# Exchange of the rotary halves: four ScalarE copies out of PSUM in place of four DMAs per half tile

## Chip, cores and metric

One Trainium2 chip, one of its cores. The time is the device time of one execution in microseconds (us); a run's time is that of the slowest core, here the only one. Each engine of the core (TensorE or PE, VectorE or DVE, ScalarE or ACT, GpSimd or POOL, and SyncE or SP, which issues the DMAs) executes its own list of instructions in order; they wait for each other by semaphores.

## What is computed

One layer of a hybrid encoder on 1024 tokens of width 1024: a mixer (window attention of 8 query heads and 2 key heads of width 64, beside a gated delta rule), cross-attention into 256 memory tokens, and a SwiGLU feed-forward net, each between norms. The change touches the rotary embedding of the queries and keys of the window attention:

```python
def _rope(x, positions):
    half = x.shape[-1] // 2                      # 32
    inv_freq = ROPE_THETA ** (-jnp.arange(half, dtype=jnp.float32) / half)
    ang = positions.astype(jnp.float32)[..., None] * inv_freq
    cos = jnp.cos(ang)[:, :, None, :]
    sin = jnp.sin(ang)[:, :, None, :]
    x1, x2 = xf[..., :half], xf[..., half:]
    return jnp.concatenate([x1 * cos - x2 * sin, x2 * cos + x1 * sin], axis=-1)
...
    aq = _rope(aq.reshape(b, s, ATTN_HEADS, ATTN_HEAD_DIM), positions)
    ak = _rope(ak.reshape(b, s, ATTN_KV_HEADS, ATTN_HEAD_DIM), positions)
    attn_o = _window_attention(aq, ak, av, attn_sink[l])
```

Each head's 64 channels are two halves of 32. Every channel is multiplied by a cosine, and the channel 32 places away, times a sine with a sign, is added.

## The kernel before

The kernel keeps activations with channels on the 128 partitions and tokens along the free axis, and works on two halves of 512 tokens (`HALF`). Weights and activations are split into a rounded part and a rest (`split`, L102 and L103), and each matrix product is three matmuls. `proj` (L263) loads one block of 128 weight columns, splits it and multiplies it with both token halves; `gemm_b` (L260) issues 24 matmuls for each half into one PSUM bank of the pool `pg`, which has three.

The first part of the kernel (to about 605 us) is the mixer. `ORDER_1` names the delta rule's projections and the inverses of its chunk triangles, whose sums run on VectorE (`base_inverse`, L510 and L512). `ORDER_2` names the stage of this case: the gate projections `G`, the level merges `L` (`levels`), the value projection `V`, the attention projections `A` and the windows `W`:

```python
ORDER_2 = "G0 G1 G2 G3 L0 L1 V A4 A0 A1 W L2 L3 W W A2 A3 W".split()
```

`A4` projects the keys, `A0` to `A3` project 128 query channels (two heads) each. `attn_proj` (L701) handles one block: for each token half VectorE multiplies the bank by the sine table into `sn` (L709) and by the cosine table into `rop` (L710). Four DMAs on SP bring `sn` to `rot` with neighbouring blocks of 32 partitions swapped (L714), since VectorE and GpSimd combine only what lies on the same partition. GpSimd adds (L715) and SP stores the sum to `d_q` or `d_k` in DRAM (L716). There are five blocks of two halves, ten rounds in all. The tiles `rop`, `rot` and `rot2` have two buffers each (`trp`). The sine table is `sinT` (L392): the sine of the angle times `rope_s`, a column of +1 and -1 that the host makes (L71).

`next_windows` starts a new window of 128 queries and finishes the one before. A window (`window`) loads keys `kr` (L610), queries `qr` (L611) and values `vr` (L613) from DRAM, splits them on ACT and GpSimd (`khi` L616, `qs` L624 and L625), forms scores (L633) with their maxima on VectorE (L635), exponentials on ACT (`sc`, L642 and L650), and in its second part transposes them (L656), splits them (`ph`, `pl`) and multiplies by the values (L661). The queries of the first eight windows come from `A0` and `A1`, those of the last eight from `A2` and `A3`.

`levels` fetches blocks of the inverses (`cz`, `cw`, L530), spreads them over tiles with ACT, VectorE and GpSimd (`m` L540, `c` L541 and L543, `D` and `Z` L553), and goes through four small products on TensorE (L569, L575), each followed by a copy on ACT (`bs` L571, `z` L580, `Z` L591) or VectorE (L592). It stores to `d_pz` (L594). When all of it is done the scan of the delta rule starts (`scan`, L749, loads at L771 and L772), interleaved with more windows by `ORDER_3`. The scan's tiles take over memory that the projections and the rotary tiles had on the right side.

Within these lists a planner decides the order: the program is traced and then each engine's instructions are put into an order by the program order, the dependences and the times that a timing model expects. The order on each engine is fixed then; on the chip an instruction whose input is late holds up everything behind it on its engine.

Of the kernel before, what the change touches and what calls it, by code (L numbers as in the profile page):

```python
# [10 lines left out]
F32 = mybir.dt.float32  # L11
# [3 lines left out]
ALU = mybir.AluOpType  # L15
# [4 lines left out]
P = 128  # L20
# [4 lines left out]
HALF = 512  # L25
# [17 lines left out]
_ROPE_AT = len(_NAMES) * P  # L43
# [3 lines left out]
def host_constants():  # L47
    i = np.arange(P)
    blk = i // 32
    a, b = i[:, None], i[None, :]  # L50
    ba, bb = blk[:, None], blk[None, :]
    tri = {
        "ident": a == b,
        "mU": a < b,
        "mL": a > b,
        "mUi": a <= b,
        "mLi": a >= b,
        "m5": (ba // 2 == bb // 2) & (ba != bb),
        "m6": ba // 2 != bb // 2,
        "ones": a + b >= 0,  # L60
    }
    out = np.zeros((P, _NCONST), np.float32)
    for n, m in tri.items():
        out[:, _AT[n]:_AT[n] + P] = m

    out[:, _AT["band0"]:_AT["band0"] + P] = np.where(b >= a, 0.0, NEG)
    out[:, _AT["band2"]:_AT["band2"] + P] = np.where(b <= a, 0.0, NEG)
    half = np.arange(32, dtype=np.float32)
    inv = np.power(np.float32(10000.0), -half / np.float32(32)).astype(np.float32)
    out[:, _ROPE_AT] = inv[i % 32]  # L70
    out[:, _ROPE_AT + 1] = np.where(i % 64 < 32, 1.0, -1.0)  # L71
    return out


# [1 line left out]
def tile_hybrid_block(  # L76
# [4 lines left out]
    g_ffn_pre, w_gate_up, w_down, g_ffn_post, consts, out, dump=None, stop=None,  # L81
):
    nc = tc.nc
    x, mem, out = x[0], mem[0], out[0]
# [23 lines left out]
    def pool(name, bufs, **kw):  # L108
        return tc.tile_pool(name=name, bufs=bufs, reuse_waits="tile", **kw)
# [37 lines left out]
    trp = p1.enter_context(pool("trp", 2, side="right"))  # L147
# [62 lines left out]
    for hf in range(2):  # L210
        hi = hx.tile([P, KT, HALF], F32R, name=f"hhi{hf}")
        lo = hx.tile([P, KT, HALF], F32R, name=f"hlo{hf}")
        for j in range(4):
# [10 lines left out]
            for kq in range(2):  # L224
# [4 lines left out]
                o = slice(4 * kq, 4 * kq + 4), slice(j * P, (j + 1) * P)  # L229
# [33 lines left out]
    def proj(src_cols, eng=None):  # L263
        whi, wlo = load_w(src_cols, KT, P, eng)
        pp = [pg.tile([P, 512], F32, tag="pg", name="pg") for _ in range(2)]
        gemm_b(whi, wlo, hT, pp)
        return pp
# [42 lines left out]
    for hf in range(2):  # L310
        pp = pg.tile([P, 512], F32, tag="pg", name="pg")
# [65 lines left out]
    sinT = rt.tile([P, S], F32, name="sinT")  # L377
    cosT = rt.tile([P, S], F32, name="cosT")
    for hf in range(2):
        sl = slice(hf * HALF, (hf + 1) * HALF)  # L380
# [320 lines left out]
    def attn_proj(ct):  # L701
        pp = proj(w_in[:, ct * P:(ct + 1) * P])
        dst = d_q[ct * P:(ct + 1) * P, :] if ct < 4 else d_k
        for hf in range(2):
            sl = slice(hf * HALF, (hf + 1) * HALF)
            rop = trp.tile([P, HALF], F32, tag="rop", name="rop")
            sn = trp.tile([P, HALF], F32, tag="rot", name="sn")
            rot = trp.tile([P, HALF], F32, tag="rot2", name="rot2")
            nc.vector.tensor_tensor(sn, pp[hf], sinT[:, sl], ALU.mult)  # L709
            nc.vector.tensor_tensor(rop, pp[hf], cosT[:, sl], ALU.mult)  # L710

            for q in range(4):
                o = 32 * (q ^ 1)
                nc.sync.dma_start(rot[32 * q:32 * q + 32], sn[o:o + 32])  # L714
            nc.gpsimd.tensor_tensor(rop, rop, rot, ALU.add)  # L715
            nc.sync.dma_start(dst[:, sl], rop)  # L716

# [13 lines left out]
    def gate_proj(h):  # L731

        pp = proj(w_in[:, 2304 + h * P:2304 + (h + 1) * P])
        for hf in range(2):
            gt = trp.tile([P, HALF], F32, tag="rop", name="gt")
            nc.scalar.activation(gt, pp[hf], AF.Silu)
            nc.sync.dma_start(d_gate[h * P:(h + 1) * P, hf * HALF:(hf + 1) * HALF], gt)

    issue(ORDER_2, {"A": attn_proj, "V": value_proj, "G": gate_proj, "L": levels, "W": next_windows})
    dump("d_q", d_q); dump("d_k", d_k); dump("d_gate", d_gate); dump("d_v", d_v)  # L740
    p1.close()
# [453 lines left out]
    def bank(name):  # L1195
        return pg.tile([P, 512], F32, tag="pg", name=name)
# [123 lines left out]
    for t in range(NT):  # L1320
        tok = slice(t * P, (t + 1) * P)
        pp = bank("pd2")
# [57 lines left out]
```

## Time and profile before

| | |
|---|---|
| median of 3 runs | 1625.35 us (1624.68 to 1629.03) |
| profiled execution, its own time | 1627.8 us |
| its span, first to last instruction | 1626.1 us |
| mean granted TensorE clock | 0.984 |
| PE busy | 1554.1 us (96%) |
| DVE busy | 940.8 us (58%) |
| ACT busy | 747.7 us (46%) |
| POOL busy | 543.8 us (33%) |

The profile is of one execution. A row of the timeline reads: start, duration, engine, line, operation, output <- input, form, count, and in brackets the idle time of the engine before it with what released it. "PEq", "SPq" and the like are the sequencers. Rows of groups give minimum, median and maximum in ns, or the busy time with the mean. PEclk is the share of full speed that TensorE's clock was granted. A busy TensorE is not one at its peak.

### The profile page before, as it was taken

To read this page: it belongs to the slowest core of one execution; us is meant where nothing else is said; L and a number is where in the kernel's file an instruction comes from. 1 tells how busy PE (TensorE), PEld (TensorE's weight loads), DVE (VectorE), ACT (ScalarE), POOL (GpSimd) and SP (SyncE) were. 2 spreads that over 40 slices of the span, in tenths; PEclk is the share of its full clock that TensorE was granted. 3 is DMA by queue.
4 is the path that set the end of the run, shared out by engine and by line. 5 is a ranking of instruction groups with operands and counts; after the bars stand their busy time and mean duration, and the time that the engine had idled before them with its cause. 6 is when DMAs were issued, how large, how long until landed. Compare 5 with 4: busy or idle time off the path is not lost.

```text
span 1626.1 us, 21448 instructions
## 1 busy us (share of the span) xinstructions
PE 1554.1 (96%) x7690; PEld 1298.7 (80%) x7690; DVE 940.8 (58%) x1431; ACT 747.7 (46%) x1518; POOL 543.8 (33%) x501
## 2 busy tenths in 40 slices
PE   6999889999899989999999999999999999999997
PEld 5878778888799868788888777788888888888886
DVE  6855986957677864543356467666545544334332
ACT  5556553236858774564436574233233222444211
POOL 2467653334336600253202221343334332321100
PEclk9999999897999999999999999999999999999999
DMA  6134158574999585354223264432322223565451
GB/s 202 41 117 129 46 176 221 140 179 124 312 300 278 179 278 183 130 194 156 66 65 117 90 199 132 130 117 80 95 79 78 89 93 119 197 220 176 141 178 71
DMA packets 267815, 240.47 MB, mean 148 GB/s; under 512 B 43176, under 2 KB 216637, under 8 KB 267709
## 3 DMA queue, kind: packets, MB, share of 16 engines
q1 hardware_dynamic: 267709, 239.11, 47.2%
q8 instruction: 60, 0.98, 0.2%
q14 instruction: 46, 0.38, 0.1%
HBM read 177.69 MB, written 58.75 MB: 145 GB/s over the span
## 4 chain that ended last, share of the span: by engine, by line
PE 67%; DVE 10%; DMA 6%; issue 3%; ACT 3%; POOL 1%; SPq 1%; POOLq 0%; ACTq 0%; DVEq 0%
PE pmg L991 10%; PE pd L1334 8%; PE pd L1310 7%; PE pE L1163 6%; PE pD L1163 6%; PE pA L1163 6%; PE pcq L260 5%; PE pB L1163 3%; PE psc L763 3%; PE pg L260 3%; DVE acc L285 1%; DVE A L512 1%; PE pcs L1072 1%; DVE tmpb L510 1%; PE pco L1098 1%
## 5 line engine op out<-in xcount | busy, mean ns | idle before, releaser
L102 ACT CAST whi<-wraw 128x1024 fp32r<-128x1024 f32 x108 | 113.3, 1050 | 153.7 <-issue 60.0
L103 POOL TENSOR_TENSOR wlo<-wraw,whi 128x1024 fp32r<-128x1024 f32 x48 | 117.9, 2457 | 165.2 <-ACT whi L102 138.2
L260 PE MATMUL pg<-hhi,whi 128*128 128x512 f32 x352 | 143.0, 407 | 0.0
L260 PE MATMUL pg<-hlo,whi 128*128 128x512 f32 x352 | 142.3, 405 | 0.0
L260 PE MATMUL pg<-hhi,wlo 128*128 128x512 f32 x352 | 142.2, 404 | 0.0
L103 DVE TENSOR_TENSOR wlo<-wraw,whi 128x1024 fp32r<-128x1024 f32 x60 | 74.5, 1243 | 82.6 <-ACT whi L102 77.5
L991 PE MATMUL pmg<-whi,b 128*128 128x512 f32 x384 | 118.4, 395 | 2.6 <-ACT whi L102 2.2
L1163 PE MATMUL pA<-s,whi 128*128 128x512 f32 x352 | 109.5, 392 | 1.4 <-ACT m L1180 1.4
L285 DVE SCALAR_TENSOR_TENSOR acc<-cp,cols,acc 128x1024 f32<-128x1024 f32 x48 | 76.0, 1586 | 34.1 <-ACT acc L283 33.5
L991 PEld LDWEIGHTS pmg<-whi,b 128*128 128x128 f32 x384 | 71.2, 188 | 17.9 <-ACT whi L102 2.7
L1240 POOL TENSOR_TENSOR act<-act,up 128x512 f32<-128x512 f32 x33 | 44.3, 1345 | 112.3 <-issue 59.0
L260 PEld LDWEIGHTS pg<-hhi,whi 128*128 128x128 f32 x352 | 68.6, 195 | 13.6 <-ACT hhi L102 0.3
L260 PEld LDWEIGHTS pg<-hhi,wlo 128*128 128x128 f32 x352 | 68.4, 194 | 13.7
L260 PEld LDWEIGHTS pg<-hlo,whi 128*128 128x128 f32 x352 | 68.2, 194 | 13.5
L1163 PEld LDWEIGHTS pA<-s,whi 128*128 128x128 f32 x352 | 65.3, 188 | 15.1 <-ACT m L1180 2.0
L991 PE MATMUL pmg<-wlo,b 128*128 128x512 f32 x192 | 71.4, 392 | 0.0
L1212 POOL TENSOR_TENSOR sr<-wraw 128x512 f32<-128x512 f32 x22 | 28.4, 1291 | 124.8 <-DMA wraw<-in_w_gate_up_dram 118.1
L1163 PE MATMUL pA<-s,wlo 128*128 128x512 f32 x176 | 68.8, 392 | 1.1 <-DVE wlo L103 1.1
L1334 PE MATMUL pd<-wdh,ath 128*128 128x512 f32 x176 | 69.5, 395 | 0.0
L1334 PE MATMUL pd<-wdl,ath 128*128 128x512 f32 x176 | 69.5, 395 | 0.0
L1334 PE MATMUL pd<-wdh,atl 128*128 128x512 f32 x176 | 69.5, 395 | 0.0
L1310 PE MATMUL pd<-dl,whi 128*128 128x512 f32 x176 | 68.5, 389 | 0.0
(387 smaller groups left out, 4177.3 us busy)
## 6 DMA issues: line engine op xcount, KB each, us to landing
wraw<-in_w_gate_up_dram SPq DMA_DIRECT2D x52, 512.0 KB, 4.1
kv<-d_kv SPq DMA_DIRECT2D x32, 512.0 KB, 6.7
wraw<-in_w_in_dram SPq DMA_DIRECT2D x22, 512.0 KB, 4.1
araw<-d_act SPq DMA_DIRECT2D x22, 512.0 KB, 3.3
draw<-in_w_down_dram SPq DMA_DIRECT2D x22, 512.0 KB, 4.7
atr<-d_act SPq DMA_DIRECT2D x16, 704.0 KB, 4.7
d_act<-act SPq DMA_DIRECT2D x40, 256.0 KB, 2.5
d_kv<-kv SPq DMA_DIRECT2D x8, 1024.0 KB, 6.2
```

Source lines behind the costliest of these rows:

```text
L102: nc.scalar.copy(hi, src)
L103: (eng or nc.vector).tensor_tensor(lo, src, f32(hi), ALU.subtract)
L260: nc.tensor.matmul(p_, w[:, k, :], ah[a][:, k, :], start=(k == 0 and i == 0), stop=(k == nk - 1 and i == 2))
L285: nc.vector.scalar_tensor_tensor(acc, cp[:, t:t + S], taps[t], acc, ALU.mult, ALU.add)
L510: nc.vector.tensor_tensor(tv, A[:, j + 1:, j:j + 1].to_broadcast([P, n, j]), A[:, j:j + 1, 0:j].to_broadcast([P, n, j]), ALU.mult)
L763: nc.tensor.matmul(out[:, d, h, :], lt[:, d, h, :], rt[:, d, h, :], start=True, stop=True)
L991: nc.tensor.matmul(pp[t], act[a][:, k, tt], w_[:, kk, :], start=(k == 0 and i == 0), stop=(k == KT - 1 and i == 2))
L1163: nc.tensor.matmul(out_, w[a][:, k, :], xx[b_][:, k, :], start=(start and k == 0 and i == 0), stop=(k == HK - 1 and i == 2), skip_group_ch ...
L1212: nc.gpsimd.tensor_tensor(s[0], b_[:, 0:HK], b_[:, HK:], ALU.add)
L1240: nc.gpsimd.tensor_tensor(o_, o_, up, ALU.mult)
L1310: nc.tensor.matmul(pps[t], a[:, tt], b_, start=(f == 0 and i == 0), stop=(f == NF - 1 and i == 2))
L1334: nc.tensor.matmul(pp, a[:, f - f0], b_[:, f], start=(f == 0 and i == 0), stop=(f == NF - 1 and i == 2))
```

## The change

The sine product and the exchange change places. ACT copies the four blocks of 32 partitions straight out of the PSUM bank into the swapped places of `rot` (L711 afterwards), VectorE forms the cosine product from the bank as before and multiplies `rot` by the sine table in place, in SBUF. The tile `sn` is gone; the tag `rot` stays in use by `value_proj`. The sign column turns, since the sine now meets the channel at its destination and no longer at its source.

```diff
     out[:, _ROPE_AT] = inv[i % 32]
-    out[:, _ROPE_AT + 1] = np.where(i % 64 < 32, 1.0, -1.0)
+    out[:, _ROPE_AT + 1] = np.where(i % 64 < 32, -1.0, 1.0)
...
         for hf in range(2):
             sl = slice(hf * HALF, (hf + 1) * HALF)
             rop = trp.tile([P, HALF], F32, tag="rop", name="rop")
-            sn = trp.tile([P, HALF], F32, tag="rot", name="sn")
             rot = trp.tile([P, HALF], F32, tag="rot2", name="rot2")
-            nc.vector.tensor_tensor(sn, pp[hf], sinT[:, sl], ALU.mult)
-            nc.vector.tensor_tensor(rop, pp[hf], cosT[:, sl], ALU.mult)
 
             for q in range(4):
                 o = 32 * (q ^ 1)
-                nc.sync.dma_start(rot[32 * q:32 * q + 32], sn[o:o + 32])
+                nc.scalar.copy(rot[32 * q:32 * q + 32], pp[hf][o:o + 32])
+            nc.vector.tensor_tensor(rop, pp[hf], cosT[:, sl], ALU.mult)
+            nc.vector.tensor_tensor(rot, rot, sinT[:, sl], ALU.mult)
             nc.gpsimd.tensor_tensor(rop, rop, rot, ALU.add)
             nc.sync.dma_start(dst[:, sl], rop)
```

## The prediction

> **What bounds the kernel now.** I read the head of the profile page first, then the engines' busy time in the stretch where the rotary work lies, then the chain of waits through that stretch, and last the single rows the change touches.
>
> ```profile
> span 1626.1 us, 21448 instructions
> PE 67%; DVE 10%; DMA 6%; issue 3%; ACT 3%; POOL 1%; SPq 1%; POOLq 0%; ACTq 0%; DVEq 0%
> ```
>
> Over the whole kernel the chain that ends last is matrix work, and ScalarE (ACT) and the SP queue hold only 3% and 1% of it. The ten rotary halves run between 300 and 390 us, so the stage decides, not the average.
>
> ```profile
> core 0: us, PE busy (x) PEld busy (x) DVE busy (x) ACT busy (x) POOL busy (x), PEclk, DMA share, GB/s
> 300.00:340.00 40.00, 38.58 (x177) 32.31 (x177) 31.48 (x57) 9.84 (x25) 16.23 (x13) 0.83 0.69 175
> 340.00:360.00 20.00, 18.47 (x100) 15.62 (x99) 11.90 (x22) 4.30 (x10) 8.75 (x7) 0.97 0.74 198
> 360.00:380.00 20.00, 18.45 (x100) 15.62 (x98) 14.33 (x34) 13.72 (x40) 9.56 (x10) 0.95 0.37 111
> 380.00:400.00 20.00, 18.66 (x90) 16.59 (x91) 16.32 (x36) 13.03 (x36) 9.71 (x9) 0.65 0.45 128
> 400.00:420.00 20.00, 16.06 (x67) 12.60 (x67) 9.02 (x24) 14.83 (x35) 6.43 (x9) 0.76 0.67 209
> 420.00:440.00 20.00, 18.16 (x135) 16.40 (x134) 14.39 (x37) 19.04 (x48) 6.96 (x7) 1.00 0.98 331
> ```
>
> Two halves of one stage. Up to 360 us TensorE is full and ACT nearly idle (9.84 of 40, then 4.30 of 20). From 360 on ACT is busy 13 to 19 us of every 20, and from 380 TensorE stands at 0.65 of its clock and then has 4 us of idle in 20: it no longer sets the pace, it waits for window attention (`next_windows`) and for the level merges (`levels`).
>
> ```profile
> 349.50 0.67 SPq L611
> 350.22 4.27 DMA qr<-d_q
> 354.56 0.63 ACT qs L624
> ...
> 376.68 2.50 ACT sc L642 x8
> 379.18 0.53 ACT Z L591 x2
> ...
> 416.37 9.60 DMA kv<-d_kv
> ```
>
> The chain goes through the load of rotated queries (`qr`) at 350, through ACT at 354 and again at 376 to 380, and leaves the stage with the scan's first loads at 416.
>
> **Removed: forty DMAs on SP, and a link in the rotary chain.**
>
> ```profile
> L714 SPq DMA_DIRECT2D rot<-sn x40: 507/586/1220, 300.7 to 385.3; - x40
> ...
> DMA to landing us min/median/max: 1.9/2.0/4.3
> ```
>
> 40 x 0.586 = 23.4 us of SP queue and 2.0 us of flight per exchange go. SP has other work behind them:
>
> ```profile
> 327.73 3.09 SPq L714 DMA_DIRECT2D rot<-sn  x4
> 330.86 0.58 SPq L530 DMA_DIRECT2D cz<-d_inv  x1
> ```
>
> Four exchanges hold the queue 3.09 us ahead of a `levels` fetch, so that fetch moves forward by up to 3 us. TensorE is busy then with projections, so I take 0, bound -3.
>
> The other gain is latency.
>
> ```profile
> 335.27 0.69 DVE L709 TENSOR_TENSOR sn<-pg,sinT 128x512 f32<-128x512 f32 x1
> ...
> 347.04 0.53 SPq L716 DMA_DIRECT2D d_q<-rop  x1
> L715 POOL TENSOR_TENSOR rop<-rop,rot x10: 1257/1290/1757, 307.0 to 388.5; 128x512 f32<-128x512 f32 x10
> ```
>
> This is the first half of the second query tile, which the first window needs: 11.8 us from sine product to store. Afterwards it is four ACT copies (2.0, below), two products of 0.69 and GpSimd's add of 1.29 (median of the ten), about 4.7 us plus queueing. I allow 5 us sooner for the `qr` load at 349.50. What waits for that load:
>
> ```profile
> ACT qs L624 <- DMA qr<-d_q: 13.8, 3, 9.5
> 355.39 0.85 PE L575 MATMUL ps<-bs,D 128*128 128x32 f32 x6 [1.16 <-ACT bs L571]
> 356.00:364.00 8.00, 7.63 (x37) 6.43 (x37) 4.30 (x13) 3.67 (x11) 3.60 (x3) 0.79 0.29 90
> ```
>
> ACT sits 9.5 us on `qs`, and copy `bs` of `levels` is queued behind it; TensorE loses 1.16 us, then 0.37 in the next 8, in which the clock of 0.79 costs 8 x 0.21 = 1.7. Together 3.2 us. I take -3. Bounds: 0, if another load is late next (the planner puts `qs` on ACT where it expects the load, so the wait can simply move), and -7, if `levels`, whose copies stand behind that wait, comes forward by the whole 5 us that the load does and 2 of the SP bound come with it.
>
> **Added: forty ScalarE copies.** No row shows a copy of 32 partitions x 512 out of PSUM, or one between partitions. Nearest rows:
>
> ```profile
> 289.85 0.58 ACT L723 COPY vT<-pg 128x512 f32<-128x512 f32 x1
> 290.33 0.58 ACT L728 COPY vt<-ptv 128x512 f32<-128x512 f32 x1
> ...
> 317.57 0.30 ACT L588 COPY Z<-z 32x128 f32<-32x128 f32 x1
> ```
>
> Start to start the full copy takes 0.48; fewer partitions don't shorten it as far as 0.30 for a quarter of the columns tells (a copy of 128 columns, mostly fixed cost). Between 0.30 and 0.58 I take 0.50, by the row with the same columns: 2.0 us per half, 20 us in all; if the shift between partitions doubled it, 40. The bank of `pp` is held 2.0 + 0.69 instead of 1.3 us, since the cosine product reads it after the copies. Three banks turn, and a half is 24 matmuls, so 1.4 us more is covered by the two halves in between.
>
> Where do they fall? The first seven halves come before 360 us and run in ACT's idle time (9.84 + 4.30 busy of 60), most of it a wait for DMA: nothing, and 2.0 us each if that cover were gone. The last three:
>
> ```profile
> L709 DVE TENSOR_TENSOR sn<-pg,sinT x3: 691/692/692, 365.3 to 378.1; 128x512 f32<-128x512 f32 x3
> ```
>
> They come between 365 and 380, where ACT is busy 13.72 of 20 and stands in the chain. Adding 3 x 2.0 makes 19.7 of 20. Behind a copy wait the exponentials (`sc`), the copies `bs`, `z`, `Z` of `levels`, and through them VectorE, TensorE and the scan's start. Bounds 0 (all in ACT's 6.3 us of gaps) and 6; doubled copies 12. Since the gaps are single waits of about a microsecond while a half needs 2.0 in one row, I take +6.
>
> **The clock.** A wait of TensorE can cost more than itself:
>
> ```profile
> 310.56 1.54 PE L569 MATMUL ps<-m,L 128*128 128x32 f32 x8 [1.14 <-DVE L L562]
> ...
> 308.00:312.00 4.00, 2.86 (x17) 2.37 (x16) 3.93 (x9) 0.27 (x1) 0.27 (x1) 0.87 0.33 110
> 312.00:324.00 12.00, 12.00 (x37) 10.07 (x37) 11.46 (x22) 2.81 (x9) 5.34 (x5) 0.50 0.61 164
> ```
>
> After 1.14 us of idle TensorE ran 12 us at half clock: 6 us lost. Six more us of ACT between 365 and 380 can start such a stretch earlier or lengthen the one at 380 to 400. Bounds 0 and +6; much of it merges with the slow stretch that is there, so +2. The Trainium skill's page "TensorE: Matmul & The Clock Gate", section "HAM oscillation — how this bites in real kernels", states that idle gaps above about 3.4 us bring the half clock; by it this term is 0 and the sum 2 us lower. The trace disagrees: the gap before this stretch was shorter, so I keep my +2.
>
> **Moved: the sine product**, from one operand in PSUM to two in SBUF, ten times.
>
> ```profile
> L709 DVE TENSOR_TENSOR sn<-pg,sinT 128x512 f32<-128x512 f32 x10 | 6.9, 689 | 4.0 <-PE pg L260 3.8
> L553 DVE TENSOR_TENSOR Z<-cz,dmask 128x512 f32<-128x512 f32 x6 | 6.8, 1135 | 0.3 <-DMA d_pz<-Z 0.2
> ```
>
> The same shape with both operands in SBUF averages 1135 ns against 689: 0.45 more, 4.5 us over ten, bounds 0 and 4.5. VectorE is nowhere full in the stretches above (at most 16.32 of 20), so I take +1. The Trainium skill's page "SBUF — State Buffer", section "Who interferes with whom", speaks against the change here: a VectorE instruction with two SBUF inputs contends with a GpSimd one that reads SBUF, and whoever is first blocks the other. By it each product would wait out the GpSimd work it meets; the mean of 1135 above agrees. The new sign of the sine table changes no instruction.
>
> **Sum.** +6 +2 +1 -3 = +6 us, on the profiled execution's own 1627.8 us (span 1626.1 and 1.7 around it): 1633.8. That execution is 2.45 above the median 1625.35, so against the runs it is about 1631.5. No change is what stays within 0.3% (4.9 us), which is about what a measurement here can tell.
>
> **Rivals.**
> - *The load decides (faster).* The whole -7 and the rest of the SP bound come in, and the copies fall into ACT's gaps (0 to +2, no clock term): about -8, 1617. For it: the 9.5 us wait, the chain through `qr`, and TensorE's 12 us at half clock near 310, which a new order may lose. Against: ACT's 13.72 us where three halves land. It decides if `qs` no longer waits over 5 us.
> - *All hidden (same).* TensorE's projections cover the first seven halves, gaps the last three, and the wait for `qr` only moves: -1 to +3, 1626. For it: TensorE busy 38.58 of 40. Against: 380 to 420, where nothing covers anything.
> - *A new half-clock stretch (much slower).* The four copies of a half are put ahead of `bs` or the weight cast, TensorE idles over 1 us while projections are still running, and another stretch like that at 312 follows: +6 +1.1 on top of +6, 1638 to 1639. It decides from an idle of about 1.1 us before 378. For it: ACT executes in order. Against: ACT is idle enough until 360.
> - *The shift is dear.* Copies between partitions take 1.0 us: +6 more on the last three halves, 1637; no row speaks for it.
>
> The planner may also put later instructions in another order; I know no row that prices this, and the range is drawn wide on that account only as far as these ends reach.
>
> **How the numbers follow.** Forecast 0.38, the load decides 0.30, all hidden 0.20, half-clock stretch 0.09, dear shift 0.03. Faster 0.30, same 0.20, slower 0.50. The range goes from 1614 (-8 with 3 us of SP gain) to 1646 (+6 +6 +4.5 with another 4 for doubled copies); the forecast's own is 1628 to 1638, from its bounds.
>
> **What would show it.** In the profile afterwards: no `rot<-sn` issues; forty ACT copies on line 711 of about 0.5 us; the sine product between 0.69 and 1.14; `qr` loads issued near 345 and the wait of `qs` for them under 5 us; ACT above 18 of 20 us in 360 to 380, with the waits for `bs`, `Z` and `ph` longer; the scan's first `kv` load at about 418 to 422. I am wrong if that load comes before 411, if ACT's copies all stand in time in which it would have waited, or if the difference arises after 600 us.

## The result and the profile after

| | before | after |
|---|---|---|
| median of 18 runs each | 1627.02 us (1619.39 to 1632.45) | 1631.16 us (1626.98 to 1637.37) |
| ratio to before, 95% interval | | 1.0027 (1.0014 to 1.0040) |
| the same, in a later comparison (12 runs, before 29) | | 1.0004 (0.9990 to 1.0019) |
| profiled execution, own time | 1627.8 us | 1629.27 us |
| ACT busy over the span | 747.7 us | 771.5 us |

The first comparison says 4 us slower, the second says no difference; their mean is +0.16%, 2.5 us. That is within the 0.3% that the prediction called no change. Its number, 1631.5, was met almost exactly in the first comparison. That it was met so closely is partly luck: the prediction set out from a time before of 1625.35, which the 18 runs put at 1627.02, so the change measured there is +4.1 us and not +6. The working behind the number did not hold. Lines behind L707 have a number one lower in the changed kernel.

The new instructions, by the groups of the tile `rot` in the changed kernel (minimum, median and maximum in ns, then the first and last start in us):

```profile
L711 ACT COPY rot<-pg x40: 574/577/581, 297.0 to 381.3; 32x512 f32<-32x512 f32 x40
L713 DVE TENSOR_TENSOR rot<-rot,sinT x10: 681/684/2104, 304.3 to 385.3; 128x512 f32<-128x512 f32 x10
L714 POOL TENSOR_TENSOR rop<-rop,rot x10: 1261/1278/1292, 305.4 to 387.4; 128x512 f32<-128x512 f32 x10
```

The shift between partitions is not dear: 0.577 us for 32 partitions, what a full copy of 128 takes (0.58 in the prediction's rows). The sine product with two operands in SBUF is no slower than the one out of PSUM in seven of the ten halves; the other three took 1.06, 1.26 and 2.10 us.

The first half of the second query tile, in the timeline of the changed kernel, from bank to load (the prediction showed 335.27 to 347.04, and the load at 349.50):

```profile
333.85 2.34 ACT L711 COPY rot<-pg 32x512 f32<-32x512 f32 x4 [1.77 <-PE pg L260]
...
339.99 0.33 SPq L715 DMA_DIRECT2D d_q<-rop  x1
342.01 0.65 SPq L611 DMA_DIRECT2D qr<-d_q  x1
```

The exchange, from its start to the store, takes 6.1 us instead of 11.8, and the load of `qr` is issued 7.5 us sooner. ScalarE's waits for that load in the changed kernel (us in all, times, longest):

```profile
ACT qs L624 <- DMA qr<-d_q: 4.7, 2, 3.7
```

It was 13.8 with a longest of 9.5. Now the stage, by windows of the changed kernel with the same columns as before:

```profile
core 0: us, PE busy (x) PEld busy (x) DVE busy (x) ACT busy (x) POOL busy (x), PEclk, DMA share, GB/s
300.00:340.00 40.00, 34.86 (x172) 28.79 (x171) 33.62 (x64) 18.88 (x41) 15.13 (x13) 0.91 0.59 154
340.00:360.00 20.00, 19.51 (x114) 16.68 (x112) 11.13 (x21) 11.26 (x24) 10.32 (x8) 1.00 0.58 158
360.00:380.00 20.00, 17.92 (x99) 14.91 (x100) 13.01 (x32) 18.42 (x47) 10.44 (x10) 1.00 0.35 110
380.00:400.00 20.00, 15.59 (x92) 13.81 (x91) 14.64 (x34) 15.86 (x42) 7.53 (x7) 0.83 0.26 81
400.00:420.00 20.00, 14.68 (x91) 11.28 (x90) 14.01 (x37) 17.50 (x43) 8.07 (x12) 1.00 0.90 275
```

ACT did go to 18.42 of 20 between 360 and 380, as the prediction said. VectorE's cosine product comes behind the copies in the program, and in the ninth half it had to wait for them (timeline of the changed kernel; "issue" says that the profile names no releaser):

```profile
370.34 2.35 ACT L711 COPY rot<-pg 32x512 f32<-32x512 f32 x4
372.77 0.69 DVE L712 TENSOR_TENSOR rop<-pg,cosT 128x512 f32<-128x512 f32 x1 [3.29 <-issue]
```

The product starts within 0.1 us of the end of the four copies, and VectorE's work for the windows stands behind it. Yet the stage ended sooner, not later. The scan's loads and its products, and the first products of the out-projection, by their groups (first and last start). Before:

```profile
L771 SPq DMA_DIRECT2D kv<-d_kv x32: 319/424/800, 411.4 to 530.5; - x32
...
L763 PE MATMUL psc<-vn,pz x128: 270/275/377, 429.1 to 557.6; 128*128 128x128 f32 x128
...
L991 PE MATMUL pmg<-whi,s x128: 387/389/497, 609.3 to 653.5; 128*128 128x512 f32 x128
```

After:

```profile
L770 SPq DMA_DIRECT2D kv<-d_kv x32: 320/425/3103, 405.8 to 525.2; - x32
...
L762 PE MATMUL psc<-vn,pz x128: 270/275/377, 423.5 to 553.8; 128*128 128x128 f32 x128
...
L990 PE MATMUL pmg<-whi,s x128: 388/390/501, 610.6 to 653.8; 128*128 128x512 f32 x128
```

Three milestones carry the rest of this text: the first load of `kv` (the scan begins), the last `psc` from `vn` (the scan ends), and the first `pmg` (the out-projection begins). The changed kernel is 5.6 us ahead at the first and 3.8 at the second; at the third it is 1.3 behind. I call the stretch from the second to the third the seam: 51.7 us before, 56.8 after. In it the value projection of the memory (`next_values`, L896), the last windows and the casts of `mraw` and of the first output weights share ScalarE.

The seam on ScalarE, first before, then after (timeline rows):

```profile
573.02 1.05 ACT L102 CAST whi<-wraw 128x1024 fp32r<-128x1024 f32 x1 [1.54 <-PE pcv L907]
576.46 1.05 ACT L102 CAST whi<-wraw 128x1024 fp32r<-128x1024 f32 x1 [2.39 <-PE pcv L907]
...
579.92 1.04 ACT L969 ACTIVATE gpost<-gpost 128x1024 f32<-128x1024 f32 x1
```

```profile
569.22 1.05 ACT L102 CAST whi<-wraw 128x1024 fp32r<-128x1024 f32 x1 [1.54 <-PE pcv L906]
574.52 1.06 ACT L968 ACTIVATE gpost<-gpost 128x1024 f32<-128x1024 f32 x1 [4.25 <-DMA gpost<-in_g_mix_post_dram]
...
577.97 1.03 ACT L102 CAST whi<-wraw 128x1024 fp32r<-128x1024 f32 x1
```

Nothing of the change is in these rows. The planner put the scaling of `gpost` one cast earlier, its load had not landed, and ACT stood 4.25 us with the cast of `whi` behind it. That load also stands in the chain of work that ended last, after but not before:

```profile
569.72 4.78 DMA gpost<-in_g_mix_post_dram
```

TensorE and its clock, after, in the timeline and in two windows:

```profile
579.05 1.56 PE L906 MATMUL pcv<-whi,mT 128*128 128x512 f32 x4 [2.57 <-ACT whi L102]
```

```profile
575.00:580.00 5.00, 2.43 (x13) 1.79 (x11) 1.31 (x3) 4.98 (x13) 0.00 (x0) 0.97 1.05 398
580.00:585.00 5.00, 5.00 (x19) 3.81 (x18) 3.73 (x5) 5.00 (x9) 0.00 (x0) 0.69 1.03 409
```

An idle of 2.57 us, then 5 us at 0.69 of the clock, worth another 5 x 0.31 = 1.6. Before, the granted clock was 1.00 over the whole seam.

### The profile page after: what moved, and what is told of

Its sections match the earlier page's. It is cut to its first block, busy times and chain, and to the rows that moved or that the text cites. A ratio compares the mean times of both kernels' runs of the same rounds, so it can differ in the third digit from the quotient of the medians.

```text
span 1627.6 us, 21405 instructions
## 1 busy us (share of the span) xinstructions
PE 1546.2 (95%) x7690; PEld 1291.5 (79%) x7690; DVE 940.9 (58%) x1431; ACT 771.5 (47%) x1558; POOL 543.1 (33%) x501
## 4 chain that ended last, share of the span: by engine, by line
PE 61%; DMA 5%; DVE 3%; ACT 3%; issue 2%; POOL 1%; SPq 0%; POOLq 0%; ACTq 0%; DVEq 0%
PE pmg L990 10%; PE pd L1333 8%; PE pd L1309 7%; PE pE L1162 6%; PE pD L1162 6%; PE pA L1162 6%; PE pcq L260 5%; PE pB L1162 3%; PE psc L762 2%; PE pcs L1071 1%; PE pco L1097 1%; DMA wraw<-in_w_gate_up_dram 1%; PE pow L661 1%; DMA wraw<-in_w_ckv_dram 1%; DMA pz<-d_pz 1%
```

## The experiments

Three theories were set against each other. *Given back at the seam*: the exchange itself costs nothing or gains, and the seam's new order loses it. *The copies cost it*: the prediction's step. *Any new order moves the time*. There are four groups of runs; every ratio is to the kernel before, run beside it.

**Is it `gpost`, and is it the order alone?** The first group took `gpost`'s scaling off ScalarE in both kernels, moved the copies to VectorE, and made a change in the kernel before that adds and removes no work.

```diff
-        nc.scalar.mul(t, t, math.sqrt(D))
+        if g is g_mix_post:
+            nc.gpsimd.tensor_scalar(t, t, math.sqrt(D), None, ALU.mult)
+        else:
+            nc.scalar.mul(t, t, math.sqrt(D))
```

> The changed kernel, with the scaling of the mixer's post-norm gains (gpost, 128x1024, one instruction) moved from ScalarE to GpSimd, so that its wait for the load at about 570 us no longer stands ahead of a weight cast on ScalarE. Theory 'given back at the seam': the exchange itself brings the scan's first kv load to about 406 us (before: 411.4) and 4 us are lost again between 570 and 610, because ScalarE waits 4.25 us for gpost's load with the cast of whi behind it. Expects the kv load at 405 to 407 as in the changed kernel, no ScalarE wait of over 1 us for gpost, the first product of the out-projection (pmg) at 606 to 608.5 instead of 610.6, and a time 2 to 4 us under the changed kernel's: 1627 to 1629, ratio to before 0.9985 to 1.001. Rival 'the copies cost it' (the prediction's step: ScalarE's 23 us of copies): the copies are untouched, so the time stays at 1630 to 1632, ratio 1.002 to 1.0035. Rival 'any new order of the plan moves the time': pmg may fall anywhere from 604 to 615 and the time with it, with no tie to gpost.

> The kernel before with the same edit: gpost's scaling on GpSimd. There ScalarE casts two whi before it comes to gpost, so 'given back at the seam' expects little: first pmg at 608 to 609.5, time within 1.5 us of before, ratio 0.999 to 1.001. 'The copies cost it' says the same. 'Any new order moves the time' expects a difference of 2 us or more in either direction, from a place that has nothing to do with gpost.

Measured: the changed kernel with it 1.0015 (1.0003 to 1.0026), seam 54.8 us (558.1 to 612.9); the kernel before with it 0.9972 (0.9954 to 0.9989), seam 49.4 (555.5 to 604.9). Both my numbers missed: the seam shrank by 2 in each, not by 2 to 4 in the one and 0 in the other. So the wait for `gpost` is part of the seam's price, and not what distinguishes the kernels by itself. The second version is the only one of the study that is clearly faster than both kernels; of the three theories only the third had expected 2 us or more of it.

```diff
-                nc.scalar.copy(rot[32 * q:32 * q + 32], pp[hf][o:o + 32])
+                nc.vector.tensor_copy(rot[32 * q:32 * q + 32], pp[hf][o:o + 32])
```

> The changed kernel with the four copies of the exchange on VectorE in place of ScalarE. 'The copies cost it': ScalarE is relieved of 23 us between 320 and 420 us, of which the prediction laid 6 on the path; expects the scan's first kv load 3 to 6 us sooner than in the changed kernel (400 to 403) and a time of 1625 to 1628, unless VectorE becomes the bound there. 'Given back at the seam': the copies stood mostly in time in which ScalarE would have waited; expects the kv load at 404 to 409, and the time follows what the plan makes of the seam at 570 to 610: gpost ahead of the cast 1630 to 1633, behind it 1626 to 1629.

Measured: 1.0073 (1.0053 to 1.0092), `kv` at 418.6 us. Both theories missed; the clause on VectorE as the bound is what happened. Windows of this run:

```profile
300.00:320.00 20.00, 18.90 (x99) 15.49 (x97) 19.64 (x31) 3.82 (x9) 8.23 (x6) 1.00 0.46 130
320.00:340.00 20.00, 16.74 (x81) 13.62 (x81) 19.08 (x38) 3.94 (x10) 3.95 (x4) 0.91 0.19 66
340.00:360.00 20.00, 16.36 (x85) 13.05 (x83) 17.11 (x27) 4.30 (x10) 9.75 (x7) 1.00 0.93 233
360.00:380.00 20.00, 16.13 (x66) 12.82 (x66) 19.46 (x41) 9.64 (x27) 9.04 (x9) 0.77 0.35 93
```

VectorE (third busy column) is full, and the same forty copies put the scan back by 13 us here, although the load of `qr` is issued as early as in the changed kernel (342.09). A useful by-product: its plan has two casts ahead of `gpost`, as before, and its seam is 52.3 us (563.8 to 616.1), before's length.

```diff
-            nc.vector.tensor_tensor(sn, pp[hf], sinT[:, sl], ALU.mult)
             nc.vector.tensor_tensor(rop, pp[hf], cosT[:, sl], ALU.mult)
+            nc.vector.tensor_tensor(sn, pp[hf], sinT[:, sl], ALU.mult)
```

> The kernel before with its two products, of sine and of cosine, in the other order on VectorE: no work more or less, the chain through the DMAs 0.7 us later per half tile, and a new order of the plan. It measures what a new order alone is worth. 'Given back at the seam' and 'the copies cost it': kv load at 411 to 413, time within 2 us of before, ratio 0.9988 to 1.0012. 'Any new order moves the time': the time moves by 2 to 5 us, with the difference arising after the exchange.

Measured: 1.0029 (1.0017 to 1.0041). The kernel before, with DMAs, no ACT copies and two neighbouring instructions swapped, loses about what the change lost in the first comparison. Its scan begins and ends as in before (`kv` 411.2, last `psc` 556.4); its seam is 57.5 us. ScalarE there:

```profile
576.54 1.05 ACT L102 CAST whi<-wraw 128x1024 fp32r<-128x1024 f32 x1 [3.69 <-PE pcv L907]
579.73 1.06 ACT L969 ACTIVATE gpost<-gpost 128x1024 f32<-128x1024 f32 x1 [2.14 <-DMA gpost<-in_g_mix_post_dram]
...
583.18 1.03 ACT L102 CAST whi<-wraw 128x1024 fp32r<-128x1024 f32 x1
```

The planner made the same choice, one cast and then `gpost`, out of an edit that leaves the exchange with the DMAs. The seam is not longer by that alone. TensorE's clock was low in it before ScalarE came to `gpost`, by 10 x 0.34 = 3.4 us of the 5.8 by which it exceeds before's:

```profile
566.40:576.40 10.00, 9.11 (x32) 7.13 (x32) 4.39 (x10) 6.03 (x17) 2.20 (x3) 0.66 0.38 112
```

**The seam pinned.** Two runs put one constraint on ScalarE's order, two put a barrier of all engines between scan and out-projection.

```diff
-        nc.scalar.mul(t, t, math.sqrt(D))
+        with (tc.issue_after(vcast[3].ins) if g is g_mix_post else ExitStack()):
+            nc.scalar.mul(t, t, math.sqrt(D))
```

> The changed kernel with one constraint on ScalarE's order: the scaling of gpost is issued after the fourth cast of the value weights (whi), so that one more cast stands ahead of it than in the changed kernel; up to there and behind it the order of every engine stays the same but for ties. 'Given back at the seam' (ScalarE's wait of 4.25 us for gpost's load delays that cast, and with it PE): kv load at 404 to 408, from the load of mraw to the first pmg 35 to 38 us instead of 40.4, time 2 to 4 us under the changed kernel's, ratio to before 0.9985 to 1.0010. Rival 'the copies cost it': nothing changes, 1.002 to 1.0035. Rival 'the seam is longer by its order, but not for gpost's sake': the stretch stays at 39 to 41 us, ratio 1.002 to 1.0035.

> The kernel before with the same constraint, which there moves the scaling of gpost behind one more cast and one mraw. 'Given back at the seam': in before the wait for gpost stood behind the casts that PE needs next, so at most 1 us is to be had: kv load at 410 to 413, stretch from mraw's load to pmg 34 to 36 us (before 35.4), ratio 0.999 to 1.001. 'Any new order moves the time': 2 us or more in either direction.

Measured: changed 1.0011 (0.9997 to 1.0024), seam 55.3; before 0.9991 (0.9978 to 1.0003), seam 49.9. From the first load of `mraw` to `pmg` the changed kernel took 38.7 us, just above the expected 35 to 38, and its ratio lies just above the expected range too, but below that of either rival. In the changed kernel TensorE's wait for that cast is gone, but only some 2 us of seam with it: a stretch of slow clock, which cost 1.6 us in the changed kernel, came later and longer (10 x 0.30 = 3 us). A window of that run:

```profile
584.70:594.70 10.00, 9.41 (x36) 7.54 (x35) 6.48 (x14) 5.90 (x14) 0.90 (x2) 0.70 1.06 370
```

```diff
     p2.close()
     p12.close()
+    tc.strict_bb_all_engine_barrier()
```

> The changed kernel with all engines waiting for each other once, where the scan's buffers are closed and the out-projection begins; so the order behind that point is the same in both kernels and nothing of the out-projection can be drawn into the scan. To be set against the next run, the kernel before with the same barrier. 'Given back at the seam': with the seam pinned the exchange shows what it brings by itself: this run 3 to 6 us under the next one, in the profile as in the times. 'The copies cost it': 3 to 7 us above the next one. 'The exchange is neutral and the 4 us at the scan's start are the clock of one profiled execution': the two within 1.5 us.

> The kernel before with the same barrier. All theories: 8 to 25 us above before, since the casts and weight loads of the out-projection no longer overlap the last steps of the scan; what counts is the difference to the run above.

Measured: 1.0106 (1.0086 to 1.0126) with the change, 1.0106 (1.0089 to 1.0124) without. By the groups, with the change:

```profile
L771 SPq DMA_DIRECT2D kv<-d_kv x32: 320/426/3078, 406.5 to 525.5; - x32
...
L763 PE MATMUL psc<-vn,pz x128: 271/275/377, 425.0 to 554.7; 128*128 128x128 f32 x128
```

and without:

```profile
L771 SPq DMA_DIRECT2D kv<-d_kv x32: 319/425/850, 409.4 to 526.5; - x32
...
L763 PE MATMUL psc<-vn,pz x128: 270/275/377, 427.4 to 554.7; 128*128 128x128 f32 x128
```

The third theory of that pair holds for the time: the exchange is neutral (medians 1646.89 and 1648.11 us). It does not hold for the scan's start, where the lead is not that of one execution, as the section on the prediction shows. Its 2.9 us there are gone at the scan's end. The intervals leave room for some 0.27% (4 us) either way, so the prediction's net +6 is outside them and a gain of 4 is only just inside.

**The seam ordered by hand, and the changed kernel again.** One run repeats the changed kernel; the other adds to the constraint on `gpost` a second one, which keeps three of the casts of `mraw` behind the fifth value cast, near the order of before.

```diff
-            split(mxT[hf][0][:, k2, :], mxT[hf][1][:, k2, :], raw[:, k2, :])
+            with (tc.issue_after(vcast[4].ins) if not hf and kp >= 1 else ExitStack()):
+                split(mxT[hf][0][:, k2, :], mxT[hf][1][:, k2, :], raw[:, k2, :])
```

> The changed kernel once more, unaltered, for a second profiled execution and for its time on the same chip as the runs beside it. All theories: ratio to before 1.001 to 1.0045. 'Given back at the seam' expects the scan's first kv load at 404 to 409 and 53 to 58 us from the last product of the scan (psc from vn) to the first pmg, as in the first profile (405.8; 56.8).

> The changed kernel with ScalarE's order at the seam set by hand to nearly that of before: gpost behind the fourth cast of the value weights (as in the run with one constraint), and of the four mraw tiles the second to fourth behind the fifth cast. The rotary exchange and everything up to 570 us stay the same. 'The seam's order costs it': from the last psc of the scan to the first pmg 49 to 53 us instead of 56.8, no stretch there under a clock of 0.9, a time 3 to 5 us under the changed kernel's on the same chip, ratio to before 0.998 to 1.001. 'The copies cost it': no change against the changed kernel, 1.002 to 1.0035.

Measured: the unaltered changed kernel 1.0004 (0.9990 to 1.0019), a little under what every theory expected; `kv` 408.4, seam 57.5 (554.7 to 612.2). Ordered by hand 0.9994 (0.9980 to 1.0008), seam 53.8 (555.9 to 609.7). The seam is 3 to 4 us shorter, a little less than expected, and it does hold a slow stretch (a clock of 0.67 from 590 to 595 us, after TensorE waited 2.62 us for a cast). The time is lower by 0.1%, where 3 to 5 us were expected, and these intervals don't tell that from nothing.

**What a copy costs.** Each copy twice, with the barrier; and the sum on VectorE.

```diff
-                nc.scalar.copy(rot[32 * q:32 * q + 32], pp[hf][o:o + 32])
+                for _ in range(2):
+                    nc.scalar.copy(rot[32 * q:32 * q + 32], pp[hf][o:o + 32])
```

> The changed kernel with the barrier between scan and out-projection, and each of the forty copies made twice: 23 us more of ScalarE between 297 and 385 us, the seam's order pinned. To be set against the changed kernel with the barrier (kv load 406.5, ratio 1.0106). 'The copies stand in time in which ScalarE would have waited': kv load at 406 to 410, ratio 1.009 to 1.0135. 'The copies cost it' (the prediction's step, by which those of the last three halves are paid in full, 6 us of 20): as much again, kv load at 412 to 418, ratio 1.014 to 1.018.

Measured: 1.0160 (1.0138 to 1.0182) against 1.0106 with single copies, so 0.54% or 8.8 us (the two intervals allow 4 to 14) for 23 us more of ScalarE. `kv` comes at 419.0 instead of 406.5, the last `psc` at 563.8 instead of 554.7. ACT's windows in this run:

```profile
320.00:340.00 20.00, 17.52 (x86) 14.48 (x85) 13.88 (x27) 17.77 (x38) 3.84 (x4) 0.91 0.65 155
...
360.00:380.00 20.00, 18.47 (x96) 15.21 (x96) 12.98 (x36) 18.01 (x44) 8.22 (x7) 0.91 0.28 80
380.00:400.00 20.00, 13.74 (x79) 12.40 (x77) 12.35 (x26) 18.53 (x43) 10.92 (x11) 0.74 0.35 101
```

Here 'the copies cost it' has its numbers, with `kv` a little above them. Of the chain of work that ended last, between 300 and 430 us, the copies are 14.4%. They also gave the earlier load away, which comes as late as before the change (342.15 us in the run with single copies):

```profile
350.00 0.64 SPq L611 DMA_DIRECT2D qr<-d_q  x1
```

So the second forty are on the path, by way of that load and otherwise, and the run doesn't tell the two apart. It says nothing of the first forty by themselves.

```diff
-            nc.gpsimd.tensor_tensor(rop, rop, rot, ALU.add)
+            nc.vector.tensor_tensor(rop, rop, rot, ALU.add)
```

> The changed kernel with the sum of the two rotated products on VectorE in place of GpSimd: ten instructions move, VectorE gets some 7 us more where it is 11 to 14 of 20 us busy (340 to 380 us), and the chain to qr gets shorter. In the plan that comes of it three casts of the value weights stand ahead of gpost on ScalarE. 'The seam's order costs it': seam of 49 to 53 us from the last psc to pmg, ratio 0.996 to 1.0005, unless VectorE delays the scan's start by more than 3 us. 'The copies cost it': 1.001 to 1.004.

Measured: 1.0010 (0.9994 to 1.0027). The seam is 53.2 us, near what was expected of it, but VectorE put the scan's start back to 412.9, by more than the 3 us that the expectation excepted, and the two about cancel.

All seams together, by kernel. The casts are those of the value weights, counted from the third of the eight, the first one in the rows above. The clock is the mean granted in the seam, and the last column is the seam times that clock, an estimate of its length without the slow stretches:

| kernel | exchange by | casts ahead of `gpost` | seam, us | clock | seam x clock |
|---|---|---|---|---|---|
| before | DMA | two | 51.7 | 1.00 | 51.7 |
| before, one constraint | DMA | three | 49.9 | 1.00 | 49.9 |
| before, scaling on GpSimd | DMA | - | 49.4 | 1.00 | 49.4 |
| before, products swapped | DMA | one | 57.5 | 0.94 | 54.1 |
| changed, twice | ScalarE | one | 56.8, 57.5 | 0.97, 0.97 | 55.1, 55.8 |
| changed, one constraint | ScalarE | two | 55.3 | 0.94 | 52.0 |
| changed, order by hand | ScalarE | two | 53.8 | 0.97 | 52.2 |
| changed, scaling on GpSimd | ScalarE | - | 54.8 | 0.94 | 51.5 |
| changed, sum on VectorE | ScalarE | three | 53.2 | 0.97 | 51.6 |
| changed, copies on VectorE | VectorE | two | 52.3 | 0.97 | 50.7 |

Two profiled executions of one order agree within 0.7 us, and the orders differ by up to 8. The three seams with one cast ahead of `gpost` are the longest, with either kind of exchange. But the place of `gpost` is not the whole of it: with that set right, the changed kernel's seam stays 2 to 4 us above before's. The clock accounts for most of that rest. In the last column the seams with one cast ahead are 54 to 56 us and all the others 49 to 52, with either kind of exchange. What starts a slow stretch, and why three of the kernels with DMAs had none, no run here shows.

## Why the prediction was right in its number and wrong in its reason

- *The copies, +6.* This step failed, by its size. It laid all of the last three halves (2.0 us each) on the path, because ACT's gaps between 360 and 380 were single waits. They were 2.34 us each, and ACT was as full as forecast, but only the ninth half's copies are found on the path, by way of VectorE, which stood 3.29 us until they were done. Two more executions with the same order (one constraint, and scaling on GpSimd) have a chain of work that can be followed through the stage: it holds the 2.4 to 2.5 us ahead of that product, and none of the copies of the eighth and tenth half. The first of them, where the four copies begin at 370.55:

```profile
370.53 2.46 issue
372.99 0.69 DVE rop L712
```

  The same chain also holds 2.35 us of copies of the sixth half (from 343.47), which the prediction laid into idle time. Against that stands ScalarE's wait for `qr`, shorter by 9.1 us; that the one outweighs the other is argued from these rows, not isolated. The prediction's own test decides against +6: the first `kv` load was to come at 418 to 422 and I was to be wrong before 411. It came at 405.8, and between 406.5 and 408.4 in five more executions whose order is that of the changed kernel, on every engine, up to behind the scan's last product.
- *The gain from an earlier `qr`, -3.* Right in mechanism, too small. The load came 7.5 us sooner, not 5, and ACT's wait for it fell by 9.1 us. Copies and gain together were put at +3 and are worth about -3 at the scan's start, as a mean: 407.2 for six executions with the changed order (405.8, 408.4, 407.0, 406.5, 407.3, 408.3), 410.6 for four that have before's order as far (411.4, 409.6, 409.4, 412.0), and the two sets don't overlap. At the scan's end the same executions have 555.3 (553.8 to 558.1) and 554.9 (551.6 to 557.6): nothing is left that shows in this scatter. How much of the zero is copies paid and how much latency gained is not separated; removing the one without the other wasn't tried.
- *The clock, +2.* Not shown as a term of the exchange. The windows at 380 and 400 had 0.65 and 0.76 before and 0.83 and 1.00 after, but the second execution of the changed kernel had 0.67 and 0.90: this differs between executions of one order. The stretch that did cost time lies at the seam: 0.69 behind an idle of 2.57 us, and 0.66 behind one of 3.14 in the second execution. The Trainium skill's page "TensorE: Matmul & The Clock Gate", section "HAM oscillation — how this bites in real kernels", puts the half clock behind idle gaps above about 3.4 us; these gaps, too, were shorter.
- *The sine product, +1.* Seven of ten took 0.68, so the 1.135 of the row it was judged by does not carry over to each. Three took 1.06, 1.26 and 2.10. Each of the three began while a GpSimd instruction was running; two of them in the timeline of the changed kernel:

```profile
303.45 1.36 POOL L553 TENSOR_TENSOR Z<-cz,dmask 128x512 f32<-128x512 f32 x1 [2.11 <-DVE Z L553]
304.30 1.06 DVE L713 TENSOR_TENSOR rot<-rot,sinT 128x512 f32<-128x512 f32 x1
...
320.37 1.91 POOL L515 TENSOR_TENSOR A<-A,bB 128x1024 f32<-128x1024 f32 x1 [2.88 <-DVE V L514]
320.73 2.10 DVE L713 TENSOR_TENSOR rot<-rot,sinT 128x512 f32<-128x512 f32 x1
```

  All three ended 0.55 us behind that instruction, which is little less than the usual 0.68, as if they had waited for it. Four others overlap with a GpSimd instruction that began after them, and took 0.68. That agrees with the Trainium skill's page "SBUF — State Buffer", section "Who interferes with whom", by which a VectorE instruction with two SBUF inputs contends with a GpSimd one that reads SBUF, and the order of issue decides who blocks. In all 2.4 us, and the longest of the three stands in both chains named above.
- *SP's queue, 0.* The forty DMAs are gone; no gain of their own was isolated.
- *The planner.* The prediction named it, found no row with a price, and gave it none. By the profiles that was the term that decided; in the times it is less sure, since the order set by hand shortened the seam by 3 to 4 us and moved the time by 0.1%. Its price is now known for one seam: 5 us of profile, slow clock included, and with the swapped products 0.29% of time, as much as the change showed at its worst. The prediction said it would be wrong if the difference arose after 600 us; it arose between 554 and 611.

Of the rivals, "the load decides" had the mechanism of the first half, its condition (`qs` waits no longer than 5 us) and its sign up to the scan's start; "all hidden" has the size of what is left.

What stays open: the change's time was measured at +0.04% and at +0.27%, with intervals from -0.10 to +0.40. In each pair of runs without a barrier the changed kernel is the slower one, by 0.43% with the scaling on GpSimd and by 0.20% with one constraint, so that a small loss that goes with the exchange is not excluded. Of the seam's 5 us the runs account for 2 (the one constraint, 55.3 against a mean of 57.2) to 3.4 (the order by hand, 53.8); that slow clock is most of the rest is an estimate, and whether it goes with the order of the window attention around it wasn't taken apart. Nor is every microsecond of seam found again in the median times, since those scatter by as much.

## What to carry to other kernels

Where a planner orders the program, compare the order of every engine far behind the edit before believing in a cause near it, and run one edit that changes no work: what it moves is the floor under which a change proves nothing. A latency taken off a chain is worth what the next join lets through, so follow it to the stage's end: here 5.7 us of exchange became 3 at the scan's start and nothing at its end. Look for room in the stage (ScalarE 9.84 of 40 us, VectorE 31.48 of 40) and not in the average: forty copies on ScalarE, with the shorter exchange, came to nothing here, forty on VectorE put the scan back by 13 us, and forty more on ScalarE cost 8.8 us of their 23. Work on one engine can be paid for on another, so ask who waits for it: here VectorE stood 3.29 us until the ninth half's copies were done.

## What was unexpected of the hardware

- Copies of 32 partitions between partitions, out of PSUM, take 0.577 us each and follow each other every 0.59 (2.34 for four), as long as one copy of 128 partitions and without the overlap that the full copies showed (0.48 from start to start).
- On VectorE the same copy takes longer, 0.686 us (median of the forty in the run with the copies there).
- One profiled execution is not the kernel: in two of the changed kernel the stretch from the first `pA` of the feed-forward to its first `pd` took 432.1 and 437.5 us with the same instructions in the same order, more than the effect under study.
